# A four-megabyte gate matrix moved from the start of a layer into its expert stream, and a reordered first projection

## The chip, the cores and the metric

The kernel runs on one NeuronCore of a Trainium2 chip. It is one program of 13,070 instructions. The metric is device time in microseconds; lower is better. Five engines work side by side: TensorE (PE in the rows, its weight loads PEld), VectorE (DVE), ScalarE (ACT), GpSimd (POOL) and SyncE (SP), which here only issues transfers. All weights come from HBM over the core's 16 DMA engines.

## The reference

One layer of a streaming encoder, batch 1, 256 tokens, width 1024, all in float32. What matters here:

```
mod = silu(c) @ w_ada + b_ada                       # w_ada: 1024 x 6144
sh1, sc1, g1, sh2, sc2, g2 = split(mod, 6)          # six vectors of 1024
h = rms_norm(x) * (1 + sc1) + sh1
proj = h @ w_in                                     # 1024 x 2216: z, xbc, dt, q, kv, k_rope
...                                                 # SSD heads, attention heads
x = x + g1 * rms_norm(mix)
h = rms_norm(x) * (1 + sc2) + sh2
f = moe(h)                                          # router, top 4 of 32 experts,
                                                    # gate_up 1024 x 2048 and down 1024 x 1024 of each expert
x = x + g2 * rms_norm(f)
```

So the columns 5120 to 6143 of `w_ada` (4 MB) make g2, which is needed only at the very end; sh2 and sc2 (columns 3072 to 5119) are needed before the router.

## The kernel before, in words

All weights pass once through SBUF. A class `Stream` holds a list of wanted tiles in the order of use and issues a load on SP's queue as soon as a buffer is free. Until the experts, tiles are single buffers `w0` to `w6` (1 MB each); afterwards two of them join to one of nine pairs (2 MB each), so that up to 18 MB are loaded ahead. `st_.take` names a tile, `st_.done` gives its buffer back and issues what waits.

The order of work before the experts: `mod_sum(0)` forms half of sh1 and sc1 on TensorE from four `w_ada` tiles, `mod_use(0)` turns it into columns and forms the modulated activations as four slices k = 0 to 3, each as a rounded part `hTh` (ACT, L521) and a rest `hTl` (DVE, L523 and L524). Weights of `w_in` are split likewise into a rounded part (ACT, L474) and a rest (DVE or POOL, L477) by `split`, and each product is three matmuls, hi by hi, hi by lo, lo by hi (`mm3`, L482 to L484). `split_xbc(q)` and `in_xbc(q)` do this for 1024 columns, `split_nat` and `in_nat` for 680 columns more; q = 0 to 3 takes two k-slices each. The first `split_xbc` is held back by `tc.issue_after` until the last slice of `mod_use(0)` has been issued.

From there to the experts TensorE's instructions are in program order (`manual_schedule`); the other engines' order comes from a planner that simulates a timeline. In that stretch `ada()` is called once per remaining `w_ada` tile: four matmuls (recorded as eight, L699) that multiply the broadcast `crep` (silu of c) with 128 rows of 2048 columns. Group r = 1 makes g1 and sh2, group r = 2 (eight tiles `ada2k`, columns 4096 to 6143) makes sc2 and g2 together.

Then 32 experts follow in a loop over `e`. Each takes four gate_up tiles and two down tiles of 2 MB. The matmuls `gu` (L1252), `py` (L1300), `pc` (L1338) and the small gathers fill TensorE. An expert with more than 64 tokens runs an extra block (`overflow`); one does. `gain()` at e = 19 multiplies g2 into the norm's gain row.

Of the kernel before, what the change touches and what calls it, by code (L numbers as in the profile page):

```python
# [19 lines left out]
D = 1024  # L20
# [47 lines left out]

RING = 7

PAIRS = (("w0", "w1"), ("w2", "w3"), ("w4", "w5"), ("w6", "x0"), ("f2", "f3"), ("f4", "f5"), ("f0", "f6"), ("f7", "f8"), ("v1", "v3"))
# [62 lines left out]
def body(ctx, tc, a, out, ne=NE):  # L134
# [218 lines left out]

    prT = tl([P, P], "prT")
    biasT = tl([P, 4 * P], "biasT")
    gate = tl([P, TT, NE], "gate")
# [21 lines left out]
    with ExitStack() as fc:  # L378
# [115 lines left out]
        mc = pn[0][:, 440:456]  # L494
        last_mod = [None]
        sums = {}
# [12 lines left out]

        def mod_use(h):  # L510
            for j in range(4):
                T.matmul(mc[:, 8 * h + 2 * j : 8 * h + 2 * j + 2], sums[h][:, j * P : (j + 1) * P], sel, start=h + j == 0, stop=True,
                         skip_group_check=True)
            half = two([P, 2, 4], "mh")
            ksl = slice(4 * h, 4 * h + 4)
            V.tensor_tensor(half, mc[:, 8 * h : 8 * h + 8].rearrange("p (k s) -> p s k", s=2),
                            prE[:, E_B1 : E_B1 + 16].rearrange("p (s k) -> p s k", s=2)[:, :, ksl], op=OP.add)
            V.scalar_tensor_tensor(a1[:, ksl], half[:, 1, :], 1.0, prE[:, E_PM + 4 * h : E_PM + 4 * h + 4], op0=OP.add, op1=OP.mult)
            for j in range(4):
                k = 4 * h + j  # L520
                A.activation(hTh[:, k, :], hT[:, k, :], AF.Identity, bias=half[:, 0, j : j + 1], scale=a1[:, k : k + 1])  # L521
                tm = v2[:, 1024 + S * (j % 2) : 1024 + S * (j % 2) + S]
                V.tensor_scalar(tm, hT[:, k, :], a1[:, k : k + 1], half[:, 0, j : j + 1], op0=OP.mult, op1=OP.add)  # L523
                last_mod[0] = V.tensor_tensor(hTl[:, k, :], tm, hTh[:, k, :], op=OP.subtract)  # L524

# [28 lines left out]

        mod_sum(0)
        mod_use(0)
        pa += [bank(f"pa{j}").rearrange("p (c s) -> p c s", c=2) for j in range(4)]
        pn += [bank("pn1", "B"), bank("pn2", "Z")]
        for q in range(4):
            if q == 0:  # L560
                with tc.issue_after(last_mod[0].ins):
                    wx = split_xbc(q)
            else:
                wx = split_xbc(q)
            wn = split_nat(q)
            in_xbc(q, wx)
            if q == 1:
                mod_sum(1)
                mod_use(1)
            in_nat(q, wn)  # L570
# [101 lines left out]
        WEIGHED = 5  # L672
        rows_left = [(1, k) for k in range(WEIGHED, KT)] + [(1, 0)] + [(2, k) for k in range(KT)]
        part_sum = {}
# [15 lines left out]
        def ada(n=1):  # L690
            for _ in range(min(n, len(rows_left))):
                r, k = rows_left.pop(0)
                if (r, k) == (1, WEIGHED) or r == 2 and k == 0:
                    mm[r] = bank(f"mm{r}", "Z")
                done = (r, k) in ((1, 0), (2, KT - 1))
                w = st_.take(f"ada{r}{k}")
                by = ones[:, 0:32] if (r, k) == (1, 0) else crep[:, k, :]
                for j in range(4):
                    T.matmul(mm[r][32 * j : 32 * j + 32, :], by, w[:, 512 * j : 512 * j + 512], start=k == (WEIGHED if r == 1 else 0), stop=done)  # L699
                st_.done(f"ada{r}{k}")  # L700
                if done:
                    ms.append(v2[:, 1024:1536] if r == 1 else tl([P, 512], "ms1", "cbs"))
                    own, oth = (slice(0, 64), slice(64, 128)) if r == 1 else (slice(64, 128), slice(0, 64))
                    V.tensor_tensor(ms[r - 1][own, :], mm[r][own, :], badd[own, :], op=OP.add)
                    A.copy(ms[r - 1][oth, :], mm[r][oth, :])

# [290 lines left out]
        def columns():  # L997

            b2 = prT[:, R_B2 : R_B2 + 16].rearrange("p (r h q) -> p r h q", r=2, h=2)
            for r in range(2):  # L1000
                b = bank("mt2", "Z")
                for q in range(4):
                    T.transpose(b[:, q * P : (q + 1) * P], ms[r][:, d_of(q)], ident)
                bv = b.rearrange("p (q j m) -> p j q m", q=4, j=4)[:, 2 - 2 * r : 4 - 2 * r, :, 0]
                V.tensor_tensor(md2[:, r, :].rearrange("p (h q) -> p h q", h=2), bv, b2[:, r], op=OP.add)
            V.scalar_tensor_tensor(a2, a2, 1.0, prT[:, R_PF : R_PF + KT], op0=OP.add, op1=OP.mult)
# [96 lines left out]
        turn_p(5)  # L1103
        ada()
        decay(1, 4)
# [329 lines left out]
    def gates_by_expert():  # L1435
# [5 lines left out]
        return gT  # L1441

    def gain():

        for h in range(2):
            sl = slice(h * 512, h * 512 + 512)
            b = mp.tile([P, 512], F32, tag="pc", name="bc", bufs=2)
            T.matmul(b, ones[64 + 32 * h : 65 + 32 * h, :], ms[1][64 + 32 * h : 65 + 32 * h, :], start=True, stop=True)
            V.tensor_tensor(end[:, sl], b, end[:, sl], op=OP.mult)
        return end[:, 0:D]  # L1450
# [30 lines left out]
    last = ne - 1  # L1481
    for e in range(ne):
        wg = weights_up(e)
        wdp, wd = wd, weights_down(e)
# [148 lines left out]
```

## Time and profile before

| | us |
|---|---|
| median of 3 runs | 1158.57 |
| lowest and highest | 1158.33 and 1159.62 |
| the profiled execution's own time | 1159.5 |
| its span, first to last instruction | 1157.7 |

| engine | busy us | share of the span |
|---|---|---|
| PE | 1069.6 | 92% |
| DVE | 419.8 | 36% |
| ACT | 191.1 | 17% |
| POOL | 69.5 | 6% |

The DMA engines moved 449.21 MB, 388 GB/s on the mean over the span. Busy time of PE is not the same as PE being the bound: matmuls are pipelined, and a stage that waits for weights can still be busy most of the time. Which resource sets the pace is read stage by stage.

### The profile page before, as it was taken

What the parts mean: (1) busy time and instruction counts of PE and PEld (TensorE: products, weight loads), DVE (VectorE), ACT (ScalarE), POOL (GpSimd) and SP (SyncE); (2) the same over time, 40 slices, a digit from 0 to 9 for tenths busy, and PEclk for the clock granted to TensorE, in tenths of its full rate; (3) what the DMA queues carried; (4) which work ended last, traced back from release to release, by engine and by line L of the source; (5) the groups of instructions that cost most, each with busy time, mean ns of one, the idle gap of its engine ahead of it and who ended that gap; (6) DMA issues with size and microseconds to landing.
All of it is one profiled execution on the core that took longest, in us unless ns stands there. A gap on an engine that the chain in (4) does not pass through costs nothing. (4 is left out here: it accounts for less than half of the span.)

```text
span 1157.7 us, 13070 instructions
## 1 busy us (share of the span) xinstructions
PE 1069.6 (92%) x5125; PEld 456.0 (39%) x5128; DVE 419.8 (36%) x892; ACT 191.1 (17%) x366; POOL 69.5 (6%) x68
## 2 busy tenths in 40 slices
PE   5999998989999999899989998999899998999996
PEld 3886674333333333333323332333323332333333
DVE  3358755333333323232322333142313232323224
ACT  5464433110111111001000101010101010101003
POOL 0274330000000000000000000000000000000000
PEclk9999999999999999899989999999989998999998
DMA  9959679968989999999999999999999999999982
GB/s 341 354 227 368 243 280 417 380 266 354 412 351 427 427 427 429 426 428 427 427 427 428 428 427 427 428 428 425 430 427 428 426 429 428 420 421 428 428 357 74
DMA packets 47713, 449.21 MB, mean 388 GB/s; under 512 B 6741, under 2 KB 11062, under 8 KB 21210
## 3 DMA queue, kind: packets, MB, share of 16 engines
q1 hardware_dynamic: 47162, 447.41, 93.0%
q8 instruction: 75, 1.23, 0.4%
q14 instruction: 60, 0.49, 0.1%
q10 hardware_dynamic: 416, 0.07, 0.0%
HBM read 446.42 MB, written 1.05 MB: 387 GB/s over the span
## 5 line engine op out<-in xcount | busy, mean ns | idle before, releaser
L1252 PE MATMUL gu<-gu,xT 128*64 128x512 f32 x2048 | 474.8, 612 | 30.5 <-DMA gu<-in_w_gate_up 28.5
L1252 PEld LDWEIGHTS gu<-gu,xT 128*64 128x64 f32 x2048 | 146.5, 140 | 308.9 <-issue 272.4
L1300 PE MATMUL py<-dn,ac 128*64 128x512 f32 x992 | 218.9, 594 | 0.2 <-DVE ac L1288 0.2
L1300 PEld LDWEIGHTS py<-dn,ac 128*64 128x64 f32 x992 | 70.7, 137 | 143.0 <-issue 133.6
L1309 DVE COPY cm<-py 64x512 f32<-64x512 f32 x30 | 20.8, 694 | 210.9 <-ACT cm L1308 210.9
L1258 DVE COPY gs<-gu 128x512 f32<-128x512 f32 x31 | 21.4, 692 | 174.9 <-PE gu L1252 174.9
L1257 ACT COPY gs<-gu 128x512 f32<-128x512 f32 x32 | 18.8, 586 | 317.5 <-PE gu L1252 317.5
L1338 PE MATMUL pc<-cm,gtm 128*128 128x512 f32 x120 | 59.3, 620 | 11.7 <-DVEq L1417 10.3
L1231 PE MATMUL pg<-x,oh 128*64 128x512 f32 x256 | 60.6, 594 | 3.6 <-DVEq L1417 1.9
L1339 DVE TENSOR_TENSOR acc<-acc,pc 128x512 f32<-128x512 f32 x64 | 44.0, 688 | 38.2 <-PE pc L1338 38.1
L1596 POOL TENSOR_TENSOR x<-x,acc 128x512 f32<-128x512 f32 x1 | 1.3, 1263 | 917.8 <-ACT acc L1595 917.8
L1241 DVE TENSOR_TENSOR xT<-pgt,md 128x512 f32<-128x512 f32 x32 | 22.1, 692 | 86.4 <-PE pgt L1239 86.4
L1279 DVE TENSOR_TENSOR u<-tp,biasT 128x512 f32<-128x512 f32 x64 | 41.5, 685 | 29.5 <-PE tp L1272 29.3
L1308 ACT COPY cm<-py 64x512 f32<-64x512 f32 x30 | 17.4, 579 | 189.6 <-PE py L1300 189.6
L1272 PEld LDWEIGHTS tp<-ident,gs 128*128 128x128 f32 x256 | 34.8, 208 | 27.8 <-ACTq L1417 16.4
L1227 DVE TENSOR_SCALAR oh<-cst,rkp,r 128x64 f32<-128x64 f32 x64 | 17.2, 311 | 76.8 <-PE pg L1231 76.8
L1272 PE MATMUL tp<-ident,gs 128*128 128x128 f32 x256 | 38.2, 290 | 6.5 <-PEq L1417 5.3
L1338 PEld LDWEIGHTS pc<-cm,gtm 128*128 128x128 f32 x120 | 19.3, 188 | 51.3 <-DVEq L1417 20.0
L1233 ACT COPY xg<-pg 128x512 f32<-128x512 f32 x32 | 18.7, 586 | 121.8 <-PE pg L1231 121.7
L1285 ACT ACTIVATE sg<-u 128x512 f32<-128x512 f32 (+1 forms) x33 | 20.4, 618 | 95.3 <-DVE u L1284 91.8
L1231 PEld LDWEIGHTS pg<-x,oh 128*64 128x64 f32 x256 | 18.1, 137 | 40.9 <-issue 39.9
L1316 DVE TENSOR_SCALAR go<-cst,rkp,gate 128x64 f32<-128x64 f32 x128 | 30.0, 308 | 0.6 <-DVEq L1417 0.6
(432 smaller groups left out, 943.3 us busy)
## 6 DMA issues: line engine op xcount, KB each, us to landing
gu<-in_w_gate_up SPq DMA_DIRECT2D x128, 2048.0 KB, 21.4
dn<-in_w_down SPq DMA_DIRECT2D x62, 2048.0 KB, 29.1
w2w<-in_w_ada SPq DMA_DIRECT2D x6, 1024.0 KB
w0w<-in_w_ada SPq DMA_DIRECT2D x5, 1024.0 KB, 6.9
w0w<-in_w_ada SPq DMA_DIRECT2D x6, 512.0 KB, 6.5
w2w<-in_w_ada SPq DMA_DIRECT2D x6, 512.0 KB
w4w<-in_w_ada SPq DMA_DIRECT2D x3, 1024.0 KB, 8.7
w4w<-in_w_out SPq DMA_DIRECT2D x3, 1024.0 KB
```

Of the source, the lines that this page charges most:

```text
L1231: T.matmul(pg[64 * h : 64 * h + 64, :], oh[:, t, :], x[:, t, h * 512 : h * 512 + 512], start=t == 0, stop=t == TT - 1)
L1241: V.tensor_tensor(xT.rearrange("p (h q) s -> p q h s", h=2), pg, a2.rearrange("p (h q) -> p q h", h=2)[:, :, :, None].to_broadcast([P, 4, ...
L1252: T.matmul(gu[h][64 * g : 64 * g + 64, :], xT[:, k, :], ws(k)[:, g * 1024 + h * 512 : g * 1024 + h * 512 + 512], start=k == 0, stop=k == K ...
L1258: copy(gs[1], gu[1])
L1272: T.transpose(tp[f // 4][:, f % 4].rearrange("p g s -> p (g s)"), gs[f // 4][:, rows_of(f % 4)], ident)
L1279: V.tensor_tensor(u[:, hs], tp[h], bv[:, hs, :, None].to_broadcast([P, 4, 2, CAP]), op=OP.add)
L1285: A.activation(sg[:, fs], u[:, fs, 0, :], AF.Sigmoid, scale=1.702)
L1300: T.matmul(py[64 * g : 64 * g + 64, :], ac[:, f, :], wd(f, ch), start=f == 0, stop=f == FT - 1)
L1309: V.tensor_copy(comb[(e & 1) ^ 1][64:128, :], py[64:128, :])
L1316: V.tensor_scalar(go[:, t, j, :], iota, rkp[:, t, ee : ee + 1], gate[:, t, ee : ee + 1], op0=OP.is_equal, op1=OP.mult)
L1338: T.matmul(pc, lhs(t, ch), rhs(ch), start=bias is None or (t, ch) != bias_left[0], stop=True)
L1339: V.tensor_tensor(acc[:, t, ch * 512 : ch * 512 + 512], acc[:, t, ch * 512 : ch * 512 + 512], pc, op=OP.add)
```

## The change

First part: the first tile of `w_in` is no longer split after the four modulated slices are made but between them. A new `split_first` gives two steps, `hi(j)` on ACT and `lo(j)` on DVE, each for one k-row of 1024 columns. `mod_use(0, between)` calls `hi(0)` ahead of the first slice, `hi(1)` behind the second, and `lo(0)`, `lo(1)` behind the rests of the first two slices; ACT and DVE run this stretch in program order. `in_first` orders the 48 matmuls so that all hi by hi of one k come first.

Second part: the load of the 1024 columns of g2 leaves group r = 2, whose eight tiles become four (`ada20`, `ada22`, `ada24`, `ada26`, each two k-rows of 1024 columns). Four calls of `ada()` are taken out. The g2 columns become two pair tiles `gate0` and `gate4` (2 MB each) wanted just ahead of expert 14's weights. `last_gate()` at e = 14 multiplies them by `crep`, which gets a tile of its own, and puts the bias rows in by two small transfers on ACT's queue. `gain()` adds the partial rows by a selection matrix.

```diff
+GATED = 14
-    for j, o in enumerate((2048, 2560, 5120, 5632)):
+    for j, o in enumerate((2048, 2560)):
         side(badd[32 * j : 32 * j + 1, :], a["b_ada"][:, o : o + 512])
...
-        for k in range(KT):
-            st_.want(f"ada{r}{k}", ld(lambda t: t, w_ada[:, k, 2048 * r : 2048 * r + 2048]))
-            some(1)
+        for k in range(0, KT, r):
+            st_.want(f"ada{r}{k}", ld(lambda t: t, w_ada[:, k, 2048:4096]) if r == 1 else ld(halves, w_ada[:, k : k + 2, 4096:5120]))
+            some(r)
...
+        if e == GATED:
+            for k in (0, 4):
+                st_.want(f"gate{k}", ld(lambda t: t.rearrange("p (k c) -> p k c", k=4), w_ada[:, k : k + 4, 5120:6144]), True)
...
+    crep = tl([P, KT, 32], "crep")
-        crep = v2[:, 1536:1792].rearrange("p (k e) -> p k e", k=KT)
...
             for j in range(4):
                 k = 4 * h + j
+                if between and j == 0:
+                    between[0](0)
                 A.activation(hTh[:, k, :], hT[:, k, :], AF.Identity, bias=half[:, 0, j : j + 1], scale=a1[:, k : k + 1])
+                if between and j == 1:
+                    between[0](1)
...
+                if between and j < 2:
+                    between[1](j)
...
+        def split_first():
+            w = st_.take("xbc0")
+            t = pair(5, "whl", F32R)
+            def hi(j):
+                A.copy(t[:, 1024 * j : 1024 * j + 1024], w[:, 1024 * j : 1024 * j + 1024])
+            def lo(j):
+                sl = slice(1024 * j, 1024 * j + 1024)
+                V.tensor_tensor(t[:, 2048:][:, sl], w[:, sl], t[:, sl], op=OP.subtract)
+            return [halves(t[:, :2048]), halves(t[:, 2048:])], (hi, lo)
+        def in_first(w):
+            for k in (0, 1):
+                for i, j in ((0, 0), (0, 1), (1, 0)):
+                    for ct in range(8):
+                        T.matmul(pa[ct // 2][:, ct % 2, :], w[i][:, k, ct * P : (ct + 1) * P], (hTh, hTl)[j][:, k, :],
+                                 start=i + j + k == 0 and ct % 2 == 0, stop=False, skip_group_check=True)
...
-        mod_sum(0)
-        mod_use(0)
+        with tc.manual_schedule(engines={mybir.EngineType.Activation, mybir.EngineType.DVE}):
+            mod_sum(0)
+            wx, between = split_first()
+            mod_use(0, between)
...
         turn_p(5)
-        ada()
         decay(1, 4)
...
         part(0, 6, "f1")
-        ada()
...
         part(2, 4)
-        ada()
-        ada()
         proj(*tiles[1], (6, 7))
...
+    def last_gate():
+        b = mp.tile([P, 512], F32, tag="pc", name="mg", bufs=2)
+        for k in range(KT):
+            w = st_.take(f"gate{k - k % 4}")
+            for h in range(2):
+                o = 64 * (k % 2) + 32 * h
+                T.matmul(b[o : o + 32, :], crep[:, k, :], w[:, k % 4 * D + h * 512 : k % 4 * D + h * 512 + 512], start=k < 2, stop=k >= KT - 2)
+        for k in (0, 4):
+            st_.done(f"gate{k}")
+        gm.append(tl([P, 512], "gm", "cbs"))
+        A.copy(gm[0], b)
+        gm.append(tl([P, 2, P], "gsel"))
+        G.memset(gm[1], 0.0)
+        for h in range(2):
+            A.dma_start(gm[0][32 * h + 1 : 32 * h + 2, :], a["b_ada"][:, 5120 + 512 * h : 5632 + 512 * h])
+            for o, n in ((32 * h, 2), (64 + 32 * h, 1)):
+                G.memset(gm[1][o : o + n, h, :], 1.0)
...
     for e in range(ne):
+        if e == GATED:
+            last_gate()
```

## Rows read from the trace of the kernel before

**Rows 1.** The page: GB/s in 40 slices; the costliest group, busy, mean, idle before.
```profile
GB/s 341 354 227 368 243 280 417 380 266 354 412 351 427 427 427 429 426 428 427 427 427 428 428 427 427 428 428 425 430 427 428 426 429 428 420 421 428 428 357 74
L1252 PE MATMUL gu<-gu,xT 128*64 128x512 f32 x2048 | 474.8, 612 | 30.5 <-DMA gu<-in_w_gate_up 28.5
```

**Rows 2.** Busy time by stretch: PE, PEld, DVE, ACT, POOL, granted clock, DMA share, GB/s.
```profile
337.00:342.00 5.00, 4.71 (x21) 1.52 (x18) 0.69 (x1) 0.59 (x1) 0.00 (x0) 1.00 0.32 98
350.00:400.00 50.00, 48.57 (x222) 17.46 (x219) 14.32 (x24) 4.13 (x7) 0.00 (x0) 1.00 1.01 428
...
1000.00:1110.00 110.00, 102.95 (x464) 37.30 (x462) 33.36 (x58) 10.00 (x17) 0.00 (x0) 0.98 1.01 426
```

**Rows 3.** SP's queue at 341 us: start, length, line, tile.
```profile
341.29 1.53 SPq L230 DMA_DIRECT2D dn<-in_w_down  x2
```

**Rows 4.** PE's waits between 185 and 482 us, the first of 18 rows.
```profile
PE pg L1231 <- DVEq L1417: 1.9, 1, 1.9
```

**Rows 5.** PE's timeline: the first and the last of twelve waits for expert weights.
```profile
483.07 6.52 PE L1252 MATMUL gu<-gu,xT 128*64 128x512 f32 x16 [1.98 <-DMA gu<-in_w_gate_up]
...
1020.42 5.35 PE L1252 MATMUL gu<-gu,xT 128*64 128x512 f32 x16 [1.94 <-DMA gu<-in_w_gate_up]
```

**Rows 6.** Timeline from 22 to 26 us, where the first slices and weights are split.
```profile
22.13 2.07 ACT L521 ACTIVATE hThl<-hT,mh,a 128x256 fp32r<-128x256 f32 x4 [1.60 <-DVE a L518]
...
22.79 0.89 DVE L524 TENSOR_TENSOR hThl<-v,hThl 128x256 fp32r<-128x256 f32 x2
...
24.11 1.97 ACT L474 CAST whl<-w4w 128x1024 fp32r<-128x1024 f32 x2
25.17 1.23 DVE L477 TENSOR_TENSOR whl<-w4w,whl 128x1024 fp32r<-128x1024 f32 x1 [0.17 <-ACT whl L474]
...
25.19 0.58 PE L482 MATMUL pa<-hThl,whl 128*128 128x256 f32 x1 [3.56 <-ACT whl L474]
```

**Rows 7.** The first `w_in` tile: its issue on SP, and its time to landing.
```profile
9.30 0.37 SPq L230 DMA_DIRECT2D w4w<-in_w_in  x1
```
```profile
w4w<-in_w_in SPq DMA_DIRECT2D x1, 1024.0 KB, 12.0
```

**Rows 8.** The same stretches as in rows 2, one us each.
```profile
18.00:19.00 1.00, 0.70 (x5) 0.15 (x6) 0.00 (x0) 0.00 (x0) 0.00 (x0) 1.00 1.04 414
...
25.00:26.00 1.00, 0.81 (x4) 0.81 (x5) 0.83 (x1) 1.00 (x2) 0.00 (x0) 0.50 1.05 386
...
28.00:29.00 1.00, 1.00 (x10) 1.00 (x10) 0.00 (x0) 0.00 (x0) 1.00 (x1) 0.96 1.04 414
```

**Rows 9.** Timeline: the next tile's rest on POOL, and its matmuls with that rest.
```profile
27.43 3.11 POOL L477 TENSOR_TENSOR whl<-w6x,whl 128x1360 fp32r<-128x1360 f32 x1 [26.98 <-ACT whl L474]
...
34.72 0.46 PE L483 MATMUL pn<-whl,hThl 128*128 128x424 f32 x1
```

**Rows 10.** PE's timeline at three of the four calls of `ada` that go.
```profile
131.86 1.06 PE L699 MATMUL mm<-w4w,v 128*32 128x512 f32 x8
132.85 1.16 PE L945 MATMUL rr<-cst,da 128*128 128x128 f32 x8
...
153.84 1.07 PE L699 MATMUL mm<-w6x,v 128*32 128x512 f32 x8
...
155.69 0.50 PE L482 MATMUL pm<-whl,mix 128*128 128x512 f32 x1
```

**Rows 11.** Timeline: VectorE behind the first of them, and PE's next stop.
```profile
134.05 0.87 DVE L947 SCALAR_TENSOR_TENSOR onxs<-rr,csa,cst 128x128 f32<-128x128 f32 x3 [0.59 <-PE rr L945]
```
```profile
140.26 2.12 PE L409 MATMUL tr<-ident,onxs 128*128 128x128 f32 x8 [0.60 <-DVE onxs L1109]
```

**Rows 12.** Stretches: the second dip of the clock, and the DMA's early full stretch.
```profile
141.00:142.00 1.00, 1.00 (x7) 1.00 (x6) 0.89 (x2) 0.44 (x1) 0.00 (x0) 0.50 1.02 426
...
147.00:148.00 1.00, 1.00 (x6) 0.83 (x5) 0.47 (x1) 0.41 (x2) 0.00 (x0) 0.72 0.14 53
```
```profile
5.00:40.00 35.00, 25.81 (x161) 17.87 (x162) 9.28 (x23) 17.58 (x25) 3.38 (x2) 0.95 1.04 388
```

More of the change, by code (lines that the diff above doesn't have):

```diff
@@ L494, in body @@
         mc = pn[0][:, 440:456]
-        last_mod = [None]
         sums = {}
@@ L508, in mod_sum, with mod_use @@
             A.copy(sums[h], b)
-        def mod_use(h):
+        def mod_use(h, between=()):
             for j in range(4):
@@ L553, in in_nat @@
                         skip_group_check=True)
-        mod_sum(0)
-        mod_use(0)
+        with tc.manual_schedule(engines={mybir.EngineType.Activation, mybir.EngineType.DVE}):
+            mod_sum(0)
+            wx, between = split_first()
+            mod_use(0, between)
+        st_.done("xbc0")
         pa += [bank(f"pa{j}").rearrange("p (c s) -> p c s", c=2) for j in range(4)]
@@ L559, in body @@
         for q in range(4):
[L560 to L563, printed above, removed]
+            if q:
                 wx = split_xbc(q)
             wn = split_nat(q)
-            in_xbc(q, wx)
+            if q:
+                in_xbc(q, wx)
+            else:
+                in_first(wx)
             if q == 1:
@@ L672, in body @@
         WEIGHED = 5
-        rows_left = [(1, k) for k in range(WEIGHED, KT)] + [(1, 0)] + [(2, k) for k in range(KT)]
+        rows_left = [(1, k) for k in range(WEIGHED, KT)] + [(1, 0)] + [(2, k) for k in range(0, KT, 2)]
         part_sum = {}
@@ L694, in ada @@
                     mm[r] = bank(f"mm{r}", "Z")
-                done = (r, k) in ((1, 0), (2, KT - 1))
+                done = (r, k) in ((1, 0), (2, KT - 2))
                 w = st_.take(f"ada{r}{k}")
-                by = ones[:, 0:32] if (r, k) == (1, 0) else crep[:, k, :]
                 for j in range(4):
+                    by = ones[:, 0:32] if (r, k) == (1, 0) else crep[:, k + (r - 1) * (j // 2), :]
                     T.matmul(mm[r][32 * j : 32 * j + 32, :], by, w[:, 512 * j : 512 * j + 512], start=k == (WEIGHED if r == 1 else 0), stop=done)
@@ L702, in ada @@
                     ms.append(v2[:, 1024:1536] if r == 1 else tl([P, 512], "ms1", "cbs"))
-                    own, oth = (slice(0, 64), slice(64, 128)) if r == 1 else (slice(64, 128), slice(0, 64))
-                    V.tensor_tensor(ms[r - 1][own, :], mm[r][own, :], badd[own, :], op=OP.add)
-                    A.copy(ms[r - 1][oth, :], mm[r][oth, :])
+                    own = slice(0, 64 if r == 1 else 0)
+                    if r == 1:
+                        V.tensor_tensor(ms[0][own, :], mm[r][own, :], badd[own, :], op=OP.add)
+                    A.copy(ms[r - 1][own.stop :, :], mm[r][own.stop :, :])
         def shared_key(t):
@@ L1003, in columns @@
                     T.transpose(b[:, q * P : (q + 1) * P], ms[r][:, d_of(q)], ident)
-                bv = b.rearrange("p (q j m) -> p j q m", q=4, j=4)[:, 2 - 2 * r : 4 - 2 * r, :, 0]
-                V.tensor_tensor(md2[:, r, :].rearrange("p (h q) -> p h q", h=2), bv, b2[:, r], op=OP.add)
+                bv = b.rearrange("p (q j m) -> p j q m", q=4, j=4)[:, :, :, 0]
+                mv = md2[:, r, :].rearrange("p (h q) -> p h q", h=2)
+                V.tensor_tensor(mv, bv[:, 2:4], b2[:, r], op=OP.add)
+                if r:
+                    V.tensor_tensor(mv, mv, bv[:, 0:2], op=OP.add)
             V.scalar_tensor_tensor(a2, a2, 1.0, prT[:, R_PF : R_PF + KT], op0=OP.add, op1=OP.mult)
@@ L1441, in gates_by_expert @@
         return gT
+    gm = []
+    def last_gate():
[15 more added lines that the diff above has]
+                G.memset(gm[1][o : o + n, h, :], 1.0)
     def gain():
@@ L1447, in gain @@
             b = mp.tile([P, 512], F32, tag="pc", name="bc", bufs=2)
-            T.matmul(b, ones[64 + 32 * h : 65 + 32 * h, :], ms[1][64 + 32 * h : 65 + 32 * h, :], start=True, stop=True)
+            T.matmul(b, gm[1][:, h, :], gm[0], start=True, stop=True)
             V.tensor_tensor(end[:, sl], b, end[:, sl], op=OP.mult)
```

2 lines of the change are left out of this document (1 added, 1 removed).

## The prediction, written before the changed kernel was timed

> **What bounds the kernel now.** I read the page first. Its line of GB/s has a ragged start, a last dip in the twelfth slice, and from the thirteenth on about 427 up to the very end [rows 1]. So there are two regimes, and a table by stretches separates them: the last hole is from 337 to 342 us (DMA engines 32% busy, 98 GB/s); from 350 to 1110 us they are at 100% and move 426 to 428 GB/s [rows 2].
>
> Next, who makes whom wait. In the hole SP sits on an expert tile whose buffer TensorE has not given back, and goes on at 341.3 us [rows 3]: TensorE sets the pace there. Its own waits say the same: between 185 and 482 us none of 18 rows names a transfer, and the longest is 1.9 us [rows 4]. After that it is the reverse. From 483 us TensorE waits twelve times for expert weights, the last time at 1020.4 us for 1.94 us [rows 5]; of 30.5 us idle ahead of the gate_up matmuls 28.5 are put down to these tiles [rows 1]. Behind the last wait TensorE runs to the end by itself.
>
> This gives a simple clock. Up to the hole at 342 us every load starts when TensorE frees a buffer, so what TensorE gains before the experts reaches the hole in full, if nothing takes it back. From the hole on there is only a pile of bytes at a fixed rate: each byte more costs its time, and the tail follows the last wait. The number wanted is therefore (time of the gate's 4 MB in the full stretch) minus (TensorE's lead when it comes to the experts). The 4 MB that the early stage no longer loads give nothing by themselves, since the DMA engines had idle room there.
>
> **The gate's bytes.** 4 MB are 4,194,304 bytes. At the 427 GB/s of the late stretch [rows 2] that is 9.8 us. But the experts' rows are 16 KB long and the gate's only 4 KB. The nearest stretch with such pieces is 5 to 40 us, where the engines are just as full and move 388 GB/s [rows 12]: 10.8 us. I take 10.5, nearer to the row with the like pieces; both ends are kept.
>
> The rate is also where a page can be held against a row. The Trainium skill (DMA: Bandwidth & Descriptors, section Where 436 GB/s comes from) says that for transfers from HBM the HBM side binds, at about 358 GB/s per core. By that the gate would cost 11.7 us and the sum below would be 1.2 us higher. The rows hold 426 to 428 for 760 us [rows 2], so here the trace disagrees, and I stay with it.
>
> **The rest of the second part.** `last_gate` is 16 matmuls of the same shape as four calls of `ada`; two calls fill 153.84 to 155.69 us, so four cost 3.7 us of TensorE [rows 10]. They stand behind a transfer that TensorE must wait for anyway: the gate's tiles lie ahead of expert 14's in SP's queue, and expert 14's matmuls, queued behind, need tiles that land still later. I cost them at nothing; if that cover were gone they would cost 3.7 us. The gate takes two of nine pairs for a while, so less is loaded ahead; TensorE is at the transfers' heels there, and this too costs nothing. Two tiny transfers on ACT's queue, about 0.4 us each to issue by the row of another issue [rows 7], the memsets on an idle POOL and one more small DVE addition in `columns` stay in the same cover or slack (at most 1 us without it).
>
> **What TensorE saves on the four calls.** The call at 131.86 us holds the next group back by 0.99 us [rows 10]. But VectorE then waits only 0.59 us for that group, and TensorE's next stop, at 140.26 us, is a wait for VectorE [rows 11], so only 0.6 arrives. The other three have plain matmuls behind them: 1.85 us for the two shown and, by the first, 1.0 for the third. Sum 3.45 us; ends 2.85 (the first is worth nothing) and 3.85 (everything).
>
> **What the first part saves.** TensorE stands 3.56 us and starts at 25.19 us, when ACT has rounded the first half of the weights, behind all four slices [rows 6]. In the new order ACT rounds them first. The tile is issued at 9.30 us and needs 12.0 to land [rows 7]: 21.3 us. Half of the two casts is 1.0 us [rows 6], so `hi(0)` ends at 22.3; the first slice takes 0.5 (2.07 for four), and TensorE starts near 22.9 or 23.0: 2.2 us earlier. The second group of eight matmuls needs the first slice's rest (DVE, half of 0.89, ready near 23.4), the third needs `lo(0)` (1.23, ready near 24.6). At full clock ten matmuls start in a us [rows 8], so a group of eight takes 0.8 us and the groups come due near 23.7 and 24.5: nothing in `in_first` waits long.
>
> There is a second gain in it. The granted clock is 1.0 until the stop and 0.50 from 25 to 26 us, the lower of its two levels, after 3.56 us of standing; a half-idle stretch from 18 to 19 us (0.70 busy) had left it at 1.0 [rows 8]. It is back at 0.96 in the us from 28 [rows 8]; the 2.8 us from 25.19 to 28 are work at half speed, so 1.4 us are lost. The new stop lasts 1.4 us, nearer to the half-idle stretch, and TensorE is at work when the clock used to fall. I take it as kept: 2.2 + 1.4 = 3.6 us. Below, 0.
>
> Does that lead survive? The next product's rest is made on POOL, from 27.43 for 3.11 us, to 30.54, and cannot come earlier because its tile lands after the first; TensorE used it at 34.72 us [rows 9], and would now want it at 31.1. That still fits, by 0.6 us, so this lead is just covered and a bigger one would not be. Later tiles follow in the same close order, which is why a loss of the whole lead is a rival below.
>
> **Sum.** 10.5 - 3.45 - 3.6 = +3.45 us on the profiled execution's 1159.5 us, 0.9 above the median of the runs, 1158.57. On the median: **1162.0 us**, 0.3% slower.
>
> **The rivals.**
>
> *The gate costs nothing, and the kernel gets faster.* This holds if the late stage is in truth TensorE's: the gate's tiles would then slip into room that a few waits leave, and the time would fall by TensorE's lead, 7.05 us, to 1151.5. For it: TensorE is busy 94% of 1000 to 1110 us [rows 2], and no wait follows 1020.4. Against it: the DMA engines have no idle share in any stretch behind 350 us, and the last wait for weights, 1.94 us, is a tie to them. It decides if the last such wait vanishes without the gate's bytes moving it, that is if more than 7 of the 10.5 us find room behind expert 14. Chance 0.08.
>
> *The second clock dip goes too, and nothing changes.* From 141 us the granted clock is 0.50 and it is on its way back in the us from 147 [rows 12]: some 6 us, which cost 3. It begins at TensorE's stop at 140.26 [rows 11]. If the shifted work keeps the clock, the lead grows to 10.05 us and the sum is +0.45: 1159.0. For it: no long stop precedes the dip. Against it: the stop stays, as VectorE sets it, and with less work for TensorE before it, it does not get shorter. Chance 0.17.
>
> *The first part's lead is lost again.* TensorE starts earlier, then waits for POOL's rest or for a later tile of `w_in`, since the DMA engines are full until 40 us [rows 12]; or ACT and DVE, bound to the written order, hold something else back. Then 10.5 - 3.45 = +7.05: 1165.6. For it: the margin of 0.6 us above. Against: the rest of the stretch up to 70 us is TensorE's own work. Chance 0.15.
>
> **How the numbers follow.** Some 0.2%, 2.3 us, is what a measurement of this kernel tells from no change. The likeliest case has 0.60; with its terms at their ends (9.8 or 10.8; 3.85 or 2.85; 3.6, or 2.2 if the clock dips after all) it spans +2.35 to +5.75, that is 1160.9 to 1164.3, and further small losses in the planner's new order may push a little past either. I give four fifths of it to slower and the rest to within the bound: 0.48 and 0.12. The lost lead adds 0.15 to slower, the second dip 0.15 to the same and 0.02 to faster, the free gate 0.08 to faster. Together faster 0.10, same 0.27, slower 0.63. The range reaches from just under the second rival, 1158.3, to just over the third, 1166.2; the first rival and a small rest above it, hardly 0.2 together, stay outside.
>
> **What would show it.** In the changed kernel TensorE should start the first `w_in` product near 23 us, with a granted clock of 1.0 from 25 to 28; it should come to the first expert matmul some 7 us earlier, and the last hole of the DMA engines should move by the same amount from 337 us. Behind it the rate should stay at 427 GB/s, TensorE should have a wait of about 10 us for the gate or for expert 14, and the last wait for weights should come near 1023.9. The prediction is wrong if the hole moves by less than 4 us or by more than 9, or if the hole moves as said and the last wait does not follow it by the gate's time; the first rival shows itself if there is no wait near expert 14 at all.

## The result and the profile after

The changed kernel took 1169.13 us (median of 4 runs, 1167.94 to 1169.40) against 1158.74 for the kernel before (4 runs): ratio 1.0088, 95% interval 1.0074 to 1.0102, so 0.88% or 10.4 us slower. The forecast was 1162.0, with a range up to 1166.2: the sign was right, the size was not. The profiled execution took 1167.94 us with a span of 1166.2, against 1157.7 before: 8.5 us between the two traces. These are accounted for below; the other 1.9 us lie between the profiled executions and the medians, and no run explains them.

The first part, timeline of the changed kernel (answers to [rows 6]):

```profile
19.13 0.59 ACT L511 COPY md<-mo 128x512 f32<-128x512 f32 x1 [3.27 <-PE mo L508]
...
20.52 1.04 ACT L550 CAST whl<-w4w 128x1024 fp32r<-128x1024 f32 x1 [0.80 <-DMA w4w<-in_w_in]
...
21.47 1.09 ACT L527 ACTIVATE hThl<-hT,mh,a 128x256 fp32r<-128x256 f32 x2
...
22.12 2.29 PE L563 MATMUL pa<-hThl,whl 128*128 128x256 f32 x9 [1.30 <-ACT hThl L527]
```

TensorE's stop is 1.30 us instead of 3.56 and it starts 3.1 us earlier (0.8 of them because this execution ran 0.8 us ahead from the start). So far the step is as forecast. The clock is not; by stretches of one us (columns as in [rows 2]; answers to [rows 8]), first one of the kernel before, then the changed kernel:

```profile
24.00:25.00 1.00, 0.00 (x0) 0.00 (x0) 0.99 (x3) 1.00 (x2) 0.00 (x0) 0.83 1.10 393
```

```profile
21.00:22.00 1.00, 0.00 (x0) 0.00 (x0) 0.60 (x3) 1.00 (x3) 0.00 (x0) 0.72 1.05 387
22.00:23.00 1.00, 0.88 (x4) 0.88 (x5) 0.90 (x2) 1.00 (x3) 0.00 (x0) 0.50 1.04 380
...
28.00:29.00 1.00, 1.00 (x10) 1.00 (x9) 1.00 (x1) 0.00 (x0) 1.00 (x1) 0.86 1.04 406
```

It falls during the shorter stop and stays at its lower level (0.50, 1.2 of 2.4 GHz) until past 28 us. Before, the fall came late in the stop, by the mean of 0.83 near 24.7 us, when TensorE had stood for some 3 us; now, by the mean of 0.72, near 21.4 us, when it had stood for some 0.6. Both places are estimates from these rows. Some six us of work now lie in the low stretch, 2.8 before. The second stop, timeline (answers to [rows 11]):

```profile
133.48 2.16 ACT L478 CAST whi<-w0w 128x512 fp32r<-128x512 f32 x4
...
136.17 0.56 ACT L741 COPY ms<-mm 128x512 f32<-128x512 f32 x1
...
136.75 1.28 ACT L376 ACT_TABLE_LOAD   x1
...
138.05 0.29 ACT L376 ACTIVATE rom<-sso,epsc 128x2 f32<-128x2 f32 x1
...
139.05 0.48 DVE L1147 TENSOR_SCALAR onxs<-onxs,ro 128x512 f32<-128x512 f32 x1
...
139.58 1.38 PE L414 MATMUL tr<-ident,onxs 128*128 128x128 f32 x8 [2.65 <-DVE onxs L1147]
```

The planner has put a cast of `w_out` (2.16 us) and a copy (0.56) ahead of the root that VectorE's scaling waits for. The stop is 2.65 us where it was 0.60, and the second dip of the clock is there as before:

```profile
141.00:142.00 1.00, 1.00 (x7) 1.00 (x7) 0.92 (x2) 0.89 (x3) 0.00 (x0) 0.50 1.03 442
```

The last hole and the stretch behind it: SP's queue, two waits of TensorE at expert 14 and its last (answers to [rows 3] and [rows 5]), and the late stretches:

```profile
337.59 1.05 SPq L231 DMA_DIRECT2D dn<-in_w_down  x2
```

```profile
599.78 3.64 PE L1487 MATMUL mg<-gate,crep 128*32 128x512 f32 x16 [4.86 <-DMA gate<-in_w_ada]
604.79 3.64 PE L1487 MATMUL mg<-gate,crep 128*32 128x512 f32 x16 [1.37 <-DMA gate<-in_w_ada]
...
1027.99 1.63 PE L1287 MATMUL gu<-gu,xT 128*64 128x512 f32 x4 [2.26 <-DMA gu<-in_w_gate_up]
```

```profile
350.00:400.00 50.00, 48.58 (x226) 18.02 (x224) 16.13 (x31) 4.13 (x7) 0.00 (x0) 1.00 1.01 426
1000.00:1110.00 110.00, 104.09 (x479) 37.35 (x477) 32.52 (x64) 11.17 (x19) 0.00 (x0) 0.98 1.01 426
```

The rate is what it was, the gate's matmuls stand behind their transfers, and the hole ends 3.70 us earlier instead of some 7: less than the 4 us that the prediction had named as a sign of being wrong. TensorE's last wait for weights ended at 1027.99 us, where the prediction has 1023.9.

**The account.** Three figures split each trace: where the hole ends (SP's row of `dn`), from there to TensorE's last wait for weights, and from there to the end of the span. From the first one the clock's part can be taken off: for each one-us row before the hole, PE busy times (1 - granted clock), summed (the row of 22 us above gives 0.88 x 0.50 = 0.44). The expectations below leave out PE's share of busy time, and so have 5.1 us for the kernel before and 6.8 for the changed one where the table has 4.8 and 6.5. Executions also start apart. TensorE's first product with the summed modulation, which comes ahead of the first of its instructions that the change moves, began at:

```profile
20.57 1.05 PE L512 MATMUL pn<-sel,md 128*128 128x2 f32 x8 [0.72 <-ACT md L508]
```

```profile
19.77 1.05 PE L516 MATMUL pn<-sel,md 128*128 128x2 f32 x8 [0.72 <-ACT md L511]
```

in the kernel before and the changed one, and between 19.72 and 20.78 us over the table. This shift is carried along: TensorE's first product `yd`, ahead of the second stop, comes, less the clock's loss, at 131.8 to 133.0 us in the seven kernels that have both parts, and 112.0 to 112.7 us after that start. So the column "less both" takes the start off too, and the work saved is read there. The last columns give the timed runs; each ratio is against runs of the kernel before beside it, whose medians were 1158.73 to 1159.38. Before, `e15_before_fills`, `e5_extra_4k` and `e6_extra_16k` have the same early stage but for the fillers, and the column less both lies between 315.3 and 316.5 for them: to about 1 us it can be read.

| kernel | clock lost before the hole | hole ends | less the loss | start | less both | to last wait | to the end | median, us | ratio |
|---|---|---|---|---|---|---|---|---|---|
| before | 4.8 | 341.29 | 336.5 | 20.57 | 315.9 | 679.13 | 137.28 | 1158.74 | |
| e15_before_fills | 0.0 | 336.41 | 336.4 | 19.92 | 316.5 | 679.32 | 137.27 | 1156.83 | 0.9978 |
| e1_first_only | 4.9 | 338.64 | 333.8 | 20.16 | 313.6 | 680.25 | 139.61 | 1159.11 | 1.0002 |
| e12_first_part_fills2 | 1.7 | 335.62 | 333.9 | 19.91 | 314.0 | 680.27 | 139.71 | 1157.90 | 0.9993 |
| e2_gate_only | 5.4 | 338.29 | 332.9 | 19.79 | 313.1 | 689.24 | 137.47 | 1170.40 | 1.0102 |
| after | 6.5 | 337.59 | 331.1 | 19.77 | 311.3 | 690.40 | 138.21 | 1169.13 | 1.0088 |
| e13_fill_first2 | 4.8 | 336.18 | 331.4 | 19.89 | 311.5 | 690.41 | 138.11 | 1166.76 | 1.0068 |
| e8_fill_second | 1.6 | 332.96 | 331.3 | 19.87 | 311.5 | 690.32 | 138.12 | 1164.91 | 1.0047 |
| e4_act_order | 1.7 | 332.69 | 331.0 | 20.78 | 310.2 | 690.65 | 138.16 | 1164.31 | 1.0054 |
| e3_gate_at_2 | 6.7 | 342.24 | 335.5 | 20.73 | 314.8 | 680.44 | 138.12 | 1162.38 | 1.0035 |
| e7_order_gate2 | 4.6 | 338.39 | 333.8 | 20.32 | 313.5 | 680.50 | 139.51 | 1158.10 | 0.9987 |
| e14_all2 | 1.6 | 334.10 | 332.5 | 20.04 | 312.5 | 681.30 | 140.00 | 1157.11 | 0.9983 |
| e5_extra_4k | 5.1 | 340.56 | 335.5 | 20.20 | 315.3 | 690.38 | 140.26 | 1171.33 | 1.0095 |
| e6_extra_16k | 3.1 | 338.81 | 335.7 | 19.72 | 316.0 | 689.21 | 139.68 | 1168.98 | 1.0081 |

Between the two traces: -0.8 (the earlier start) - 4.6 (work saved up to the hole) + 1.7 (clock) + 11.3 (hole to last wait) + 0.9 (tail) = +8.5 us.

### The profile page after: what moved, and what is told of

Its sections match the earlier page's. It is cut to its first block, busy times and chain, and to the rows that moved or that the text cites. A ratio compares the mean times of both kernels' runs of the same rounds, so it can differ in the third digit from the quotient of the medians.

```text
span 1166.2 us, 13073 instructions
## 1 busy us (share of the span) xinstructions
PE 1072.1 (92%) x5125; PEld 457.8 (39%) x5128; DVE 423.1 (36%) x892; ACT 191.8 (16%) x367; POOL 72.4 (6%) x73
## 3 DMA queue, kind: packets, MB, share of 16 engines
HBM read 446.42 MB, written 1.05 MB: 384 GB/s over the span
## 5 line engine op out<-in xcount | busy, mean ns | idle before, releaser
L1293 DVE COPY gs<-gu 128x512 f32<-128x512 f32 x31 | 21.4, 691 | 175.6 <-PE gu L1287 175.6
```

Of the source, the lines that this page charges most:

```text
L1293: copy(gs[1], gu[1])
```

## The experiments

**Each part alone.** `e1_first_only` has the hunks of `split_first`, `in_first` and the order written out by hand; `e2_gate_only` has all the others.

> The first part alone on the kernel before; g2 stays where it was. Theory A (the time is the gate's transfer minus TensorE's lead at the last hole of the DMA engines, and the first part's lead shrank to about 1.3 us because the granted clock fell anyway): 1.0 to 1.8 us faster than before, first expert matmul and the hole near 341 us earlier by the same. Rival B (the prediction's own sizing, lead 3.6 us): 3 to 4 us faster. Rival C (the lead is lost by the experts): within 0.5 us of before.

Measured: 1159.11 us, ratio 1.0002 (0.9992 to 1.0012). The first product started at 22.52 us, the clock fell all the same from 22 to 26, and of the 2.6 us that the hole came earlier (0.4 of them an earlier start) nothing reached the end. The expected gain was missed; the time is that of rival C, though the lead was lost behind the hole and not ahead of the experts.

> The second part alone on the kernel before: g2's columns are loaded and used at expert 14, the first part is as before. Theory A: the transfer costs 10.9 us in the stream, the three later calls of ada and a part of the first give 2.0 us: 8 to 10 us slower than before, hole near 341 us about 2 us earlier. Rival B (the calls give 3.45 us, gate 10.5): 7 us slower. If the calls give nothing, 11 us slower.

Measured: 1170.40 us, 1.0102 (1.0087 to 1.0117). Before the hole this part saves 2.8 us of work (315.9 to 313.1); behind it, it costs 10.1 (689.24 against 679.13). The profiled execution was the fastest of the five, 1166.76 us, and 7.3 us longer in span than the kernel before's; the median is 11.4 us slower, above the 8 to 10 expected. The split holds for the profiled execution, and what the other four lost besides is not shown.

**The gate's place.**

```diff
-GATED = 14
+GATED = 2
```

> The changed kernel with the gate's loads and last_gate at expert 2 in place of expert 14; same bytes, same instructions. Theory A (bytes are dear only behind the last hole of the DMA engines at 338 us; ahead of it TensorE sets the pace and the engines have idle room): the transfer is hidden, last_gate's 3.7 us of TensorE are paid, the lead of 3.3 us is kept: between 1 us faster and 3 us slower than before, that is 7 to 10 us faster than with expert 14. Rival D (the 4 MB cost their time wherever they stand among the experts): as the changed kernel, 8 to 10.5 us slower than before. Rival E (the cost is the extra work in last_gate and gain, or the tail): also as the changed kernel.

Measured: 1162.38 us, 1.0035 (1.0021 to 1.0049), 6.75 us under the changed kernel. That is a little less gain than the 7 to 10 us expected, but rivals D and E, no gain at all, are out. The stretch behind the hole is back at 680.4. The gate now costs 3.5 us ahead of the hole (314.8 against 311.3), where TensorE sets the pace and its 3.7 us of matmuls count.

**The order on ACT.**

```diff
-        A.activation(m, ss, AF.Sqrt, bias=epsc, scale=1.0 / width)
+        roots[name] = A.activation(m, ss, AF.Sqrt, bias=epsc, scale=1.0 / width)
...
-                    A.copy(ms[r - 1][own.stop :, :], mm[r][own.stop :, :])
+                    with tc.issue_after(roots["ro" if r == 2 else "rq"].ins):
+                        A.copy(ms[r - 1][own.stop :, :], mm[r][own.stop :, :])
...
-        part(0, 6, "f1")
+        with tc.issue_after(roots["ro"].ins):
+            part(0, 6, "f1")
```

> The changed kernel, with the first w_out cast and the copy of group r = 2 queued on ACT behind the square root of the attention norm, where the planner had put them ahead of it. Theory F (these two, 2.7 us, are what made TensorE stand 2.65 us at the transposes of the attention output): that stop shrinks below 1 us, the lead at the first expert matmul grows from 3.3 to between 4.5 and 6 us, and the time falls by 1.2 to 2.7 us against the changed kernel, to 6.5 to 9 us slower than before. Rival G (the stop comes from DVE or from the clock): no change against the changed kernel.

Measured: 1164.31 us, 1.0054 (1.0036 to 1.0071): 4.8 us under the changed kernel, more than expected. Timeline of this kernel at the stop:

```profile
134.10 1.28 ACT L378 ACT_TABLE_LOAD   x1
...
136.40 1.50 DVE L1152 TENSOR_SCALAR onxs<-onxs,ro 128x512 f32<-128x512 f32 x1
...
136.53 0.33 PE L416 MATMUL tr<-ident,onxs 128*128 128x128 f32 x1
...
137.95 0.98 PE L416 MATMUL tr<-ident,onxs 128*128 128x128 f32 x7 [1.09 <-DVE onxs L1152]
```

The first transpose waits for nothing, the others 1.09 us, and the granted clock is 1.00 in each us from 139 to 150. The hole:

```profile
332.69 1.47 SPq L231 DMA_DIRECT2D dn<-in_w_down  x2
```

In the table the hole less the clock's loss is 331.0, as in the changed kernel (331.1), but this execution started 1.0 us later; less both it is 310.2 against 311.3. So the shorter stop gave 1.1 us by itself, about as much as the table can tell, and the clock the larger part, 4.8 us; of these 1.4 lie in the first dip, which this edit does not touch. That reading needed a test of its own.

**The stop filled, the order left.** TensorE transposes the identity 15 times in the stop; VectorE is as late as in the changed kernel.

```diff
+        def fill(dst, n):
+            for _ in range(n):
+                T.transpose(dst, ident, ident)
...
                 b = bank("tr", tag)
+                if k0 == 0:
+                    fill(b[:, :P], filled)
...
-        transpose_rows(on, 4, ev_mix(4, R_MN), "A")
+        transpose_rows(on, 4, ev_mix(4, R_MN), "A", filled=15)
```

> The changed kernel with 15 transposes of the identity on TensorE in its stop ahead of the transposes of the MLA output (136.9 to 139.6 us in the changed kernel); their results are overwritten. The order on ACT is not touched, so VectorE is as late as in the changed kernel and the stop's time is still lost. Theory (the second clock dip follows from the stop): the granted clock stays 1.0 from 139 to 150, the first expert matmul comes some 3 us earlier than 186.75, the hole 3 us earlier than 337.59, time 1166. Rival (the dip has another cause, such as the load of the whole stretch): the dip comes all the same, and the time stays at 1169.

Measured: 1164.91 us, 1.0047 (1.0035 to 1.0060); its interval lies below the changed kernel's. PE's timeline at the stop, and a stretch where the clock had been 0.50:

```profile
134.19 1.81 PE L408 MATMUL tr<-ident 128*128 128x128 f32 x15
137.01 1.38 PE L420 MATMUL tr<-ident,onxs 128*128 128x128 f32 x8 [1.01 <-DVE onxs L1153]
```

```profile
143.00:144.00 1.00, 1.00 (x6) 0.77 (x6) 0.25 (x2) 0.83 (x4) 1.00 (x2) 1.00 0.02 8
```

The useful work waits as long as before, 2.8 us from 134.2 to 137.0, and the time is, within the intervals, that of the repaired order. Less both, the hole is at 311.5 us, where the changed kernel has 311.3: the fillers shortened nothing, and what they gave is the clock. In this one execution the first dip was missing too, with the same instructions as the changed kernel's up to there, and a dip that cost 1.6 us came at 180 us. One profile is one draw.

**The price of bytes alone.** The kernel before, with two loads that nothing reads; `e6_extra_16k` takes `w_gu[0][:, k // 4]` in their place, the first two tiles of expert 0.

```diff
+        if e == 14:
+            for k in (0, 4):
+                st_.want(f"more{k}", ld(lambda t: t.rearrange("p (k c) -> p k c", k=4), w_ada[:, k : k + 4, 5120:6144]), True)
...
```

> The kernel before, with two more loads of 2 MB ahead of expert 14 in the queue (the same 4 KB rows of w_ada as the gate's) that no instruction reads; each gives its buffer pair back at once. Nothing else changes, and the early stage keeps its four calls. Theory A (behind the last hole every byte costs its time): 10.8 us by the early stretch's 388 GB/s, 9.8 by the late stretch's 427; so 1168.8 to 1169.8 us, with the hole at the same place (341 us) and the last wait for weights some 10 us later than 1020.4. Theory B (the late bytes find room, and the change lost its time by the order on ACT and VectorE): under 3 us, 1159 to 1162.

> As the run with 4 KB rows, but the two loads of 2 MB that nobody reads are expert-like tiles in rows of 16 KB (expert 0's first gate_up tile twice). Theory A with a price by row length: 9.8 us at 427 GB/s, 1168.8 us, about 1 us less than the run with 4 KB rows. If row length doesn't matter here, both give the same. Theory B: under 3 us.

Measured: 1171.33 us, 1.0095 (1.0078 to 1.0113), and 1168.98 us, 1.0081 (1.0065 to 1.0096). SP's queue and PE's timeline in the run with 4 KB rows:

```profile
566.77 15.15 SPq L230 DMA_DIRECT2D more<-in_w_ada  x2
```

```profile
612.22 1.12 PE L1255 MATMUL gu<-gu,xT 128*64 128x512 f32 x2 [14.54 <-DMA gu<-in_w_gate_up]
```

Theory A holds: from hole to last wait the two take 11.2 and 10.1 us longer than the kernel before. The 1.2 us by which 4 KB rows are dearer agree with the expectation, but the timed intervals overlap, and the gate itself, in the same 4 KB rows, cost 10.1 us as the 16 KB rows did: a price by row length is not shown. Some 0.8 us of both times is the tail's, by a changed order on VectorE (see below).

**Both repairs.**

> The changed kernel with both repairs: the ACT order of e4_act_order and GATED = 2 instead of 14, so that the gate's 4 MB come ahead of the last hole. If the two are independent, e4_act_order and e3_gate_at_2 add up: 1169.1 - 4.8 - 6.75 = 1157.6 us, the hole near 337.3, the last wait near 1017.6, no second dip of the clock at 141 us. Rival: the gate's earlier tiles meet the same stop again, the lead of the ACT order is lost to them, and the time is e3_gate_at_2's, 1162.

Measured: 1158.10 us, 0.9987 (0.9977 to 0.9998). The sum of the two came out within 0.5 us, so they are independent as far as the times tell. In the traces too the order on ACT is worth about the same beside either place of the gate: 1.1 us less both with expert 14, 1.3 with expert 2 (314.8 to 313.5).

**The first stop filled.** Three runs with four transposes ahead of the modulation's use and eight behind it.

```diff
             mod_sum(0)
+            with tc.issue_after(lastmm[0].ins):
+                fill(pn[0][:, :P], 4)
...
+                with tc.issue_after(lastmm[0].ins):
+                    fill(pa[3][:, 0, :P], 8)
                 in_first(wx)
```

> The changed kernel with TensorE kept at work in its first stop: four transposes of the identity behind the sum of the modulation and eight between its use and the first w_in product (about 0.12 us each by e8_fill_second, where fifteen took 1.81); their results are overwritten. The rows of the profile so far give a reading of the clock: summed over one-us rows, the clock lost before the hole is 5.1 us of full speed in the kernel before, 6.8 in the changed one, and 1.7 to 6.8 in the others. Theory (a stop of TensorE lets the clock fall): the first dip (3.4 of the 6.8 us) is gone, the hole comes some 3 us earlier than 337.59, and the time is 1166. Rival (the dip is there in any case, at random): the clock falls between 21 and 28 us all the same in the profile, and the time stays at 1169.

> The first part of the change alone (the gate's loads stay where they were), with both stops filled: twelve transposes of the identity at the first one, five (about 0.6 us) ahead of the transposes of the MLA output. Taking the clock's loss off the place of the hole, the first part alone came 2.6 us earlier than the kernel before (338.64 - 5.1 against 341.29 - 5.1). Theory: the early loss falls from 5.1 us to 0 to 1.7, so the hole comes at 333.5 to 335.2, 6 to 8 us earlier than before; the bytes behind it are those of before, and the last wait and the end follow: 1151 to 1153 us. If the dips in the tail (1.7 us each) take their share as in e1_first_only, 1154.5. Rival (dips not tied to the stops): 1159, as e1_first_only.

> The changed kernel with the order repaired on ACT, the gate at expert 2 and both stops filled (twelve transposes of the identity at the first, eight at the second). e7_order_gate2 measured 1158.1 and lost 5.1 us to the clock before the hole, 3.4 of them in the first dip. Theory: the first dip goes, so 1154.7. Rival: the second stop of this order is only some 1.1 us and its clock was already whole, so the eight transposes take time (1.0 us) and the first dip stays: 1159.

Measured: 1177.90 us (1.0163, 1.0150 to 1.0177), 1165.48 (1.0053, 1.0038 to 1.0067) and 1166.83 (1.0064, 1.0042 to 1.0085): all slower than the kernels they were made from. The clock did what the theory said, 1.00 in every us from 19 to 40 in all three. But twelve instructions more had moved the planner's order: a copy on ACT came ahead of two casts (42.94 against 43.72 us in `e9_fill_first`; 44.14 against 41.69 in the changed kernel), and so it went on behind. The PE timeline of `e9_fill_first` shows the price:

```profile
62.08 0.78 PE L492 MATMUL pn<-whl,hThl 128*128 128x424 f32 x3 [0.99 <-ACT whl L484]
...
66.41 0.39 PE L494 MATMUL pa<-hThl,whl 128*128 128x256 f32 x1 [2.17 <-DVE whl L487]
```

The hole less the clock's loss went to 339.8, 341.4 and 340.5, that is 7 to 9 us later. As tests of the clock's worth these runs fail; that the fillers keep the clock at this stop, they show. It fell elsewhere: from 144 us in `e9_fill_first`, which has the second stop of 2.65 us, and from 51 and 68 us in the other two, and the loss before the hole was 4.4, 4.9 and 3.4 us in all.

**The same with the order kept.** Eight transposes at the first stop leave the orders on ACT, VectorE and POOL as they were. `e15_before_fills` fills the stops of the kernel before (16 and 5) and has no part of the change.

> The changed kernel with eight transposes of the identity in its first stop and nothing else; all orders but TensorE's are those of the changed kernel. Theory: the clock stays 1.0 from 20 to 30 us, the hole comes 3.4 us earlier than 337.59, time 1165 to 1166. Rival (a dip comes anyway a little later, and is only moved): 1169.

> The first part alone again, with both stops filled, but with fewer transposes: eight at the first stop, five ahead of the transposes of the MLA output. With these numbers the orders on ACT, VectorE and POOL are those of e1_first_only (in e10_first_part_fills the twelve had moved four entries on ACT, and that order cost more than the clock gave). Theory (a stop lets the clock fall; behind the hole all is as before): loss of clock before the hole 0 to 1.7 us, hole 6 us or more earlier than 341.29, time 1152 to 1155. Rival (the lead does not reach the end): 1159.

> e7_order_gate2 (order repaired on ACT, gate at expert 2) with eight transposes in the first stop, other orders unchanged. Theory: 1158.1 less the first dip's 3.4 us: 1154.7, hence faster than both kernels. Rival (with the hole nearly closed in e7_order_gate2 the early stage is bound by its loads as well, so the lead is not worth its full time): 1157.

> The kernel before with its own two stops filled: sixteen transposes of the identity (1.9 of 3.56 us) ahead of the first w_in product, five (0.6 us) ahead of the transposes of the MLA output. Theory: of the 5.1 us of clock lost before the hole 3.4 to 5.1 stay, the hole comes that much earlier than 341.29, and the time falls to 1154 to 1156: as much as the first part was forecast to bring, without it. Rival (the dips are not tied to the stops here, or the fillers delay the work behind them): 1159.

Measured: `e13_fill_first2` 1166.76 us (1.0068, 1.0047 to 1.0089), just above the 1165 to 1166 expected and 2.4 under the changed kernel, though the intervals overlap; its first dip was gone and its second was longer, 136 to 147 us. `e12_first_part_fills2` 1157.90 (0.9993, 0.9981 to 1.0006), a miss: the hole came 5.7 us earlier, but see the tail below. `e14_all2` 1157.11 (0.9983, 0.9970 to 0.9997), a miss of 1154.7 and the time of its rival; in its profile, as in that of `e12_first_part_fills2`, the first dip came in spite of the eight transposes, at 1.6 and 1.7 us lost. `e15_before_fills` 1156.83 (0.9978, 0.9967 to 0.9989): faster than both kernels, by two stops filled with work that is thrown away. Its granted clock at places where the kernel before has 0.50, and its last wait:

```profile
25.00:26.00 1.00, 0.94 (x8) 0.74 (x7) 1.00 (x2) 1.00 (x2) 0.00 (x0) 1.00 1.04 385
140.00:141.00 1.00, 1.00 (x12) 1.00 (x11) 1.00 (x3) 1.00 (x5) 0.00 (x0) 1.00 1.07 459
```

```profile
1015.73 0.65 PE L1262 MATMUL gu<-gu,xT 128*64 128x512 f32 x2 [2.04 <-DMA gu<-in_w_gate_up]
```

The hole and the last wait come 4.9 and 4.7 us earlier than before: the clock's 4.8 us, to within what the table can tell. The median fell by less, 1.9 us beside its own runs of the kernel before (1158.73), and missed the 1154 to 1156 expected. The profiled execution was the fastest of the twelve. That executions differ in their dips would explain both; one profile of each kernel does not show it.

## Why the prediction was wrong, point by point

**The model held.** "Up to the hole TensorE, behind it bytes" is what every row of the table shows: hole to last wait is 679 to 681 us without the 4 MB and 689 to 691 with them.

**The gate's bytes (10.5) were sized right.** Three pairs give them alone: `e2_gate_only` against before 10.1, after against `e1_first_only` 10.15, `e13_fill_first2` against `e12_first_part_fills2` 10.1. That is 4.19 MB at 415 GB/s, between the two rows I had set as bounds. By the 358 GB/s of the Trainium skill (DMA: Bandwidth & Descriptors, section Where 436 GB/s comes from) the estimate would have been 11.7; the runs decide against that figure here.

**The work saved before the hole was sized right, but the longer second stop took a part of it back.** The figures are differences in the column less both. The start of the first part: forecast 2.2, measured 2.3 to 2.5 (`e1_first_only` against before, `e12_first_part_fills2` against `e15_before_fills`). The four calls: forecast 3.45, measured 2.3 to 2.8 in the planner's order (the three pairs above) and 3.4 with the order on ACT repaired (`e4_act_order` against `e1_first_only`). Together the forecast was 5.65; the changed kernel has 4.6, and with the order repaired 5.7. The third rival, a lead lost to POOL's rest, is not what happened: the first part's lead was still there at the hole.

**The step that failed is "I take it as kept".** I read from the rows of before that 3.56 us of standing lowers the clock and a half-idle us does not, and put 1.30 us on the safe side. The clock fell, earlier, and more work lay in the low stretch: instead of 1.4 us gained on the clock, 1.7 were lost, 3.1 us of the 5.05 by which the traces miss the sum. This was a single execution's dip taken for a property of the stop's length; even the place was misread, as the clock had fallen before the stop's end. Over the profiles, the first dip came in 9 of 10 without a filler, with stops of 1.3 and of 3.56 us alike, in 2 of 3 with eight transposes in it, and in none of 4 with twelve or sixteen. That the one profile of the changed kernel had the dip is chance in part: `e8_fill_second`, with the same instructions up to there, had none.

**The second dip.** The rival had it go away, and I had argued that the stop stays. It stayed and grew to 2.65 us, since four loads fewer bring a `w_out` tile earlier and the planner, not the diff, then queued its cast ahead of the root. The tile was asked for at 107.75 us; before, the third of `w_out` was asked for at 132.99. `e2_gate_only` has the same 2.65 us and `e1_first_only` 0.60, so it is the second part's doing. I had not looked at what earlier tiles do to ACT's order. The dip at this stop came in 5 of 5 profiles with 2.65 us, 3 of 4 with 0.60, none of 3 with the repaired order and none of 5 with fillers. The clock's price here was paid by the kernel before too, so it explains why the rival did not come true and not the distance to 1162. The longer stop itself cost 1.1 us at the hole, the difference between the changed kernel and `e4_act_order`, and that is part of the distance: a second step that failed, as the prediction says "the stop stays" and has no price for a longer one. The first expert matmul shows it more clearly; in the changed kernel and in `e4_act_order`:

```profile
186.75 1.51 PE L1287 MATMUL gu<-gu,xT 128*64 128x512 f32 x6 [1.51 <-DVE xT L1277]
```

```profile
181.55 1.94 PE L1291 MATMUL gu<-gu,xT 128*64 128x512 f32 x8 [1.51 <-DVE xT L1281]
```

Less both, that is 160.5 and 159.1 us. The three kernels with the repaired order have 158.8 to 159.1, the other four with both parts 160.4 to 161.1.

**What I had not counted, 2.05 us.** Of these, 0.9 lie in the tail: VectorE's queue has the last product of `act` ahead of one addition to `acc`, again by the planner. PE's timeline of the kernel before, then of the changed kernel:

```profile
1106.84 2.33 PE L1338 MATMUL pc<-cm,gtm 128*128 128x512 f32 x4 [1.03 <-DVE acc L1339]
```

```profile
1114.44 1.13 PE L1373 MATMUL pc<-cm,gtm 128*128 128x512 f32 x2 [1.03 <-DVE acc L1374]
1116.37 1.13 PE L1373 MATMUL pc<-cm,gtm 128*128 128x512 f32 x2 [0.80 <-DVE acc L1374]
```

The second wait is not in the kernel before, nor in `e2_gate_only`, `e10_first_part_fills` and `e15_before_fills`, which keep its order there, and it is in all the others, also in `e5_extra_4k` and `e6_extra_16k`, which have no part of the change. So it goes with the order and not with the change as such; it was read, not tried by itself. The rest, 1.15 us from hole to last wait, comes with the first part; it is 0.95 to 1.16 in three pairs of kernels (`e1_first_only` against before, after against `e2_gate_only`, `e12_first_part_fills2` against `e15_before_fills`); its cause stays open. With the 1.1 that the longer stop took back, the gate's term 0.4 too high and the 0.8 of earlier start, the sum closes: 3.1 + 2.05 + 1.1 - 0.4 - 0.8 = 5.05. All but the 0.4 and the 1.1 are differences of the same two traces, so that the sum closes proves little; the 1.1 comes from another pair, and it is what the work fell short of the forecast by (5.65 against 4.6).

**Why the first part brought nothing at the end**, with the clock kept or not: of its 2.3 us at the hole, 1.1 go back behind it and 0.8 in the tail, and in `e1_first_only` and `e12_first_part_fills2` a dip in the tail takes 1.6 more. Stretches of `e1_first_only` behind two stops of 1.05 and 0.84 us:

```profile
1080.00:1081.00 1.00, 1.00 (x5) 0.39 (x6) 0.09 (x1) 0.59 (x1) 0.00 (x0) 0.56 0.96 410
1081.00:1082.00 1.00, 1.00 (x6) 0.32 (x4) 0.00 (x0) 0.00 (x0) 0.00 (x0) 0.50 1.00 426
```

The same stops are in the kernel before (1.04 and 0.84 us), where the clock stayed at 1.00:

```profile
1082.00:1083.00 1.00, 1.00 (x7) 0.29 (x4) 0.00 (x0) 0.35 (x1) 0.00 (x0) 1.00 1.04 442
```

What decides that, these runs do not tell.

## What to carry to other kernels

Take the clock's loss off a milestone before comparing two traces, and the shift with which the execution started: work saved and clock lost are then separate columns, and each can be forecast alone. A stop that gets shorter is not a stop that keeps the clock; if TensorE must stand, throw-away matmuls in the gap are worth trying first (here 0.22% with sixteen and five transposes, more than the first part of the change brought; eight at the first stop were not enough in two profiles of three). And when loads leave a stage, read which tiles land earlier and which queue their casts will enter: a planner reorders by that, and by a dozen fillers too.

## What the runs showed of the hardware that was not expected

The granted clock fell to its lower level behind a stop of 0.60 us (three profiles of four) and in or behind stops of 1.3 us (five of six), and at the same instructions in one execution and not in the next. One execution of the kernel before lost 4.8 us so ahead of the hole, one of the changed kernel 6.5.

In `e4_act_order` one VectorE scaling of 128x512 took 1.50 us where the changed kernel's took 0.48; POOL was subtracting from 136.16 to 137.61 at that time. In `e7_order_gate2` and `e14_all2` the same scaling took 1.49 us, beside the same subtraction. The gain of the earlier root was partly lost to that.
